# An eight-core decoder layer: norm steps at an even rate, weight copies paused in two stages, and stores moved to ScalarE's queue

## The chip, the cores and the metric

The kernel runs on all 8 cores of one Trainium2 chip. The sequence of 8192 tokens is cut into 8 parts, and each core computes the whole layer for its 1024 tokens (plus a small halo). The cores don't talk to each other. The metric is the device time of the slowest core, in microseconds (us). Cores 0 to 3 are one die, 4 to 7 the other.

In some of its executions this program has a second, slower state: the cores of one die, or of both, show a lower granted TensorE clock (the share of full speed that the chip allows TensorE; no view here shows more than 1.00) and the time is longer. Fast runs are compared with fast runs here. TensorE = PE in the profile (PEld its weight loads), VectorE = DVE, ScalarE = ACT, GpSimd = POOL, SyncE = SP. A name such as ACTq is the queue of that engine in which DMAs are issued. A DMA lands when the profile shows it done; "us to landing" counts from its issue. PSUM (`ps` in the profile) is the memory into which TensorE's matmuls write here, in banks that VectorE and ScalarE then read (892 and 291 instructions in the two largest such groups of the kernel before).

## The reference, cut to what matters

```python
for i in range(DEPTH):                                # DEPTH = 1, D_MODEL 4096, D_FF 11008
    h = rms_norm(x, norm_mix_pre[i]);  z = h @ w_in[i]
    q, k, v, u, g_attn, g_pool = jnp.split(z, split_points, axis=-1)
    # ... attention with window 128, pooling mixer ...
    merged = jax.nn.sigmoid(g_attn) * y_attn + jax.nn.sigmoid(g_pool) * y_pool
    x = x + rms_norm(merged @ w_out[i], norm_mix_post[i])             # output projection, norm, residual
    h = rms_norm(x, norm_ffn_pre[i])
    up = causal_depthwise_conv(h @ w_up[i], conv_w[i], conv_b[i])     # up-projection
    gate, val = jnp.split(up, 2, axis=-1)
    x = x + rms_norm((jax.nn.gelu(gate, approximate=True) * val) @ w_down[i], norm_ffn_post[i])
    ple_gate = jax.nn.sigmoid(rms_norm(x, norm_ple_gate[i]) @ w_ple_gate[i])      # the gate
    x = x + rms_norm(ple_gate * (p[i] @ w_ple[i]), norm_ple_post[i])
```

Inputs and output are fp32; the kernel multiplies in bf16 and accumulates in fp32. Each `x = x + rms_norm(...)` is a run of 32 norm steps, one for each block of 128 channels.

## The kernel before

The kernel is a list of jobs, which are matmul groups over one output block of 128 channels. Near the output projection, the down-projection's end and the gate, each stage is cut into two parts of tokens: "part 0" (the first 512) and "part 1". While TensorE works on one part, the norm steps of the other are put between its matmuls. A queue named `side` holds these steps, and a job takes one off it after every `side` matmul groups:

```python
            cnt = 0                                    # in run_jobs, anew for every job
            ...
                    cnt += 1
                    if side and cnt // side > (cnt - 1) // side and self.side:
                        self.side.popleft()()
```

So with 32 groups per job and `side` 12, a job takes 2 steps, and the remaining 8 groups are forgotten. What is left in the queue runs in one lump at `B.code(B.drain_side)`.

One norm step, cut:

```python
        def main(k):
            m, x, r = src[k], S["x"][k % NR], S["r"]          # NR = 4 buffers for the residual
            O("dve", "tensor_tensor", ..., out=m.v, in0=m.v, in1=r, op=ALU.mult)
            O("dve", "scalar_tensor_tensor", ..., in1=x.v, ...)   # gain, plus the residual x
            ld_(k + NR)                                       # SyncE: next residual load
            put(k, m)                                         # SyncE: store of the new x (or of out)
            if hout is not None:
                O("act", "activation", ..., func=AF.Square)   # q
                O("act", "activation", ..., func=AF.Copy)     # h, input of the next matmuls
        def step(k):
            def run():
                if k < NCH:
                    main(k)
                if hout is not None and k >= 2:
                    ss(k - 2)                                 # TensorE: sum of the squares of step k - 2
```

Weights come in slabs of up to 8 x 128 x 128, which GpSimd loads as bf16 into a ring of 12 (`sb_wr`). Beside the slabs GpSimd also issues copies: weights that are read twice are turned from fp32 in memory (`w_out`, ...) to bf16 in memory (`b_out`, ...), one copy of 1 MB for every 8 slabs:

```python
        self.O("pool", "dma_start", [cast] if cast else [], [self.wringB[i]], dma=f"wr{i}", ...)
        if self.casting and self.nload % 8 == 0:
            self.cast_next()
```

All waits are worked out from reads and writes. A write marked `partial` still waits for every earlier writer of the same record, and all stores to `out` share one record (`outB`) and one counter:

```python
        for b in writes:
            for d in (b.w, b.r):                  # also with partial=True
                for k, v in d.items():
                    deps[k] = max(deps.get(k, 0), v)
    ...
    O("sp", "dma_start", [m.b], [outB], partial=True, dma="out", out=out_d[k][:, t0:t0 + 512], in_=m.v)
```

The gated mixer tiles `mg` that did not fit into on-chip memory are loaded back by SyncE at the end of the mixer gates, once `h0` and `r0` are free.

The softmax here doesn't subtract the row's maximum and nothing guards it: scores larger than these inputs give would overflow.

## Time and profile before

| | before |
|---|---|
| runs beside the changed kernel | 7069.54, 7080.66, 7090.2 us fast; 7908.45 slow |
| profiled run, spans of the cores | 7037.4 to 7086.9 us, core 7 slowest |
| mean granted clock | 0.966 to 0.972 |
| TensorE busy (core 7) | 6628.3 us, 94% |
| DMA moved (core 7) | 910.65 MB |

The lines of this profile stand in the prediction below.

### The profile page before, as it was taken

Reading aid. Unit: us, or ns where it says so; the run is one execution under the profiler, and the core shown is the slowest. Engines: PE = TensorE matmul, PEld = TensorE weight load, DVE = VectorE, ACT = ScalarE, POOL = GpSimd, SP = SyncE. Lnnn points to the kernel's source line nnn. Section 1 sums busy time; section 2 is a strip of 40 time slices with the busy share of each in tenths; the row PEclk is TensorE's granted clock in tenths of the full one; section 3 lists DMA queues with packets and bytes.
Section 4 is the critical chain, followed back from the end, with each engine's and each line's share of the span. In section 5 each row is a group of like instructions: output and inputs, shape, how many; then the busy total and the mean of one; then the engine's idle time right before and its main releaser. Section 6 shows DMA issues by size and latency. Waiting matters only on the chain.

```text
span 7086.9 us, 104514 instructions; the slowest of 8 cores (7037.4 to 7086.9 us)
## 1 busy us (share of the span) xinstructions
PE 6628.3 (94%) x41282; PEld 4048.3 (57%) x41282; DVE 1984.6 (28%) x2553; ACT 823.3 (12%) x1242; POOL 1335.2 (19%) x2501
## 2 busy tenths in 40 slices
PE   5999999999999787899999999999999999997865
PEld 3656666666664563666654566664456666443332
DVE  3343211111110213433310133331023333244334
ACT  2550000000001222100000000000000000133111
POOL 1111111111113222211111111111111111332321
PEclk8999999999999888899999999999999999998987
DMA  6457877777789999844456644447864444686563
GB/s 162 77 80 109 119 113 114 120 117 118 114 150 207 203 198 196 174 76 76 76 102 118 114 76 76 76 76 141 160 114 76 76 76 93 203 267 206 163 205 120
DMA packets 377375, 910.65 MB, mean 128 GB/s; under 512 B 50176, under 2 KB 72960, under 8 KB 371328
## 3 DMA queue, kind: packets, MB, share of 16 engines
q0 software_dynamic: 289344, 705.33, 57.3%
q1 hardware_dynamic: 87552, 198.64, 9.2%
q8 instruction: 337, 5.52, 0.3%
q14 instruction: 142, 1.16, 0.1%
HBM read 1297.47 MB, written 200.32 MB: 211 GB/s over the span
## 4 chain that ended last, share of the span: by engine, by line
PE 86%; DMA 9%; DVE 2%; ACT 1%; issue 1%; POOL 0%; DVEq 0%; SPq 0%; ACTq 0%; POOLq 0%
PE ps L143 86%; DMA sb_arena<-xr 5%; DVE sb_arena L143 2%; DMA out<-sb_arena 1%; ACT sb_arena L143 1%; DMA sb_arena<-w_in 1%; DMA sb_arena<-x_s 1%; DMA sb_wr<-b_out 1%; DMA sb_arena<-mg_s 1%; DMA sb_arena<-xs 0%; POOL sb_arena L143 0%; DVEq L142 0%; ACT L143 0%; ACTq L142 0%; SPq L143 0%
## 5 line engine op out<-in xcount | busy, mean ns | idle before, releaser
L143 PE MATMUL ps<-sb_arena,sb_wr 128*128 128x512 bf16 (+5 forms) x39744 | 6440.1, 324 | 101.3 <-DVE sb_arena L143 79.0
L143 PEld LDWEIGHTS ps<-sb_arena,sb_wr 128*128 128x128 bf16 x39744 | 3906.6, 99 | 2549.7 <-issue 137.0
L143 DVE TENSOR_TENSOR sb_arena<-ps,sb_arena 128x512 f32<-128x512 f32 (+9 forms) x892 | 682.1, 765 | 4066.7 <-PE ps L143 3868.9
L143 ACT ACTIVATE sb_arena<-sb_arena 128x512 f32<-128x512 f32 (+10 forms) x683 | 493.0, 725 | 4921.1 <-DVE sb_arena L143 4803.9
L143 POOL DMA_DIRECT2D sb_wr<-w_up x632 | 333.7, 528 | 1839.7 <-PE ps L143 1715.3
L143 DVE TENSOR_TENSOR sb_arena<-sb_arena 128x512 f32<-128x512 f32 (+8 forms) x543 | 452.0, 841 | 546.8 <-ACT sb_arena L143 518.9
L143 DVE SCALAR_TENSOR_TENSOR sb_arena<-sb_arena,sb_convp 128x1024 f32<-128x1024 f32 (+2 forms) x372 | 447.9, 1204 | 39.5 <-DVE sb_arena L143 0.9
L143 POOL DMA_DIRECT2D sb_wr<-w_in x384 | 204.3, 533 | 1308.6 <-PE ps L143 1308.6
L143 PE MATMUL ps<-sb_arena,sb_ones_b 128*128 128x296 bf16 (+3 forms) x288 | 87.4, 389 | 243.7 <-ACT sb_arena L143 217.8
L143 POOL DMA_DIRECT2D sb_wr<-w_down x256 | 135.2, 528 | 675.1 <-PE ps L143 624.1
L143 ACT ACTIVATE sb_arena<-ps 128x512 bf16<-128x512 f32 (+7 forms) x291 | 159.8, 549 | 788.6 <-PE ps L143 782.1
L143 DVE SCALAR_TENSOR_TENSOR sb_arena<-sb_arena,sb_gains 128x512 f32<-128x512 f32 (+1 forms) x192 | 144.7, 753 | 283.2 <-DMA sb_arena<-xr 204.0
L143 POOL DMA_DIRECT2D sb_wr<-b_out x256 | 138.2, 540 | 443.2 <-PE ps L143 440.2
L143 PE MATMUL ps<-sb_arena 128*128 128x296 bf16 (+4 forms) x1216 | 183.6, 273 | 27.5 <-DVE sb_arena L143 16.2
L143 POOL DMA_DIRECT2D sb_wr<-b_pg x256 | 137.4, 537 | 358.3 <-PE ps L143 342.7
L143 PEld LDWEIGHTS ps<-sb_arena,sb_ones_b 128*128 128x128 bf16 x288 | 27.3, 105 | 293.7 <-issue 282.7
L143 POOL DMA_DIRECT2D sb_wr<-b_down x256 | 137.4, 537 | 281.2 <-PE ps L143 245.1
L143 PEld LDWEIGHTS ps<-sb_arena 128*128 128x128 bf16 (+1 forms) x1216 | 110.3, 100 | 105.7 <-issue 71.2
L143 DVE TENSOR_SCALAR sb_arena<-sb_arena,sb_convp 128x1024 f32<-128x1024 f32 (+2 forms) x186 | 143.8, 773 | 20.9 <-DVE sb_arena L143 0.9
L143 POOL DMA_DIRECT2D sb_wr<-b_up x112 | 60.6, 541 | 239.0 <-PE ps L143 239.0
L143 ACT ACTIVATE sb_arena<-sb_arena,sb_gains 128x512 bf16<-128x512 f32 (+1 forms) x128 | 90.7, 708 | 0.0
L143 POOL DMA_DIRECT2D sb_wr<-w_bp x64 | 33.8, 528 | 194.2 <-PE ps L143 190.7
(34 smaller groups left out, 390.7 us busy)
## 6 DMA issues: line engine op xcount, KB each, us to landing
sb_wr<-w_up POOLq DMA_DIRECT2D x632, 256.0 KB, 4.3
sb_wr<-w_in POOLq DMA_DIRECT2D x384, 256.0 KB, 5.5
sb_wr<-b_out POOLq DMA_DIRECT2D x256, 256.0 KB, 11.9
sb_wr<-b_pg POOLq DMA_DIRECT2D x256, 256.0 KB, 3.0
sb_wr<-w_down POOLq DMA_DIRECT2D x192, 256.0 KB, 4.1
sb_wr<-b_down POOLq DMA_DIRECT2D x192, 256.0 KB, 3.8
b_out<-w_out POOLq DMA_DIRECT2D x32, 1024.0 KB, 13.0
b_pg<-w_pg POOLq DMA_DIRECT2D x32, 1024.0 KB, 18.5
```

The source lines that it names most:

```text
L143: inst = getattr(engine, fn[0])(**fn[1])
```

## The change

The intent is to keep TensorE from standing behind norm steps: no lumps, no weight copies beside the residual traffic of the two stages where it is dense, and SyncE's queue freed of stores. The diff, cut to its core:

```diff
@@ run_jobs
+        self.due = 0
-            cnt = 0
-                    cnt += 1
-                    if side and cnt // side > (cnt - 1) // side and self.side:
-                        self.side.popleft()()
+                    if side:
+                        self.due += 1 / side
+                        if self.due >= 1:
+                            self.due -= 1
+                            if self.side:
+                                self.side.popleft()()
@@ last mixer gate
-                                O("sp", "dma_start", [mgdB[c]], [t.b], ...)
+                                O("sp" if c % 2 else "pool", "dma_start", [mgdB[c]], [t.b], ...)
@@ evac of out_job, down_part and e_job (three places)
+                    B.drain_side()
                     B.side.extend(bar1(hf, G["acc"]))
@@ put of bar1, bar2 and last
-                O("sp", "dma_start", [m.b], [x1B[hf][k]], ...)
+                O("act", "dma_start", [m.b], [x1B[hf][k]], ...)
@@ before the output projection, and after the partial up-projection
+        B.code(casting(False))
...
+        B.code(casting(True))
@@ after down_part(1, ...), after the gate's part 0 and after its part 1
-        B.code(B.drain_side)
@@ tail
-                O("sp", "dma_start", [m.b], [outB], partial=True, dma="out", ...)
+                O("sp" if f % 2 else "act", "dma_start", [m.b], [outB], partial=True, dma="out", ...)
```

Half of the `mg` loads move to GpSimd. And the record `outB` stays, so each store to `out` still waits for the one before it, whichever queue it stands in.

More of the change, by code (lines that the diff above doesn't have):

```diff
@@ L268, in load_next @@
         self.nload += 1
+        assert cast is None or cast.w, wname
         src = self.dram[wname][off:off + nk * 16384].rearrange("(p m) -> p m", p=128)
@@ L733, in evac @@
                             if c in mgdB:
-                                O("sp", "dma_start", [mgdB[c]], [t.b], dma=f"mgl{c % 8}", out=t.v, in_=mg_d[c])
+                                O("sp" if c % 2 else "pool", "dma_start", [mgdB[c]], [t.b], dma=f"mgl{c % 8}", out=t.v, in_=mg_d[c])
             B.one(B.chunk(banks, NCH, rhs_e, rb_h0, evac), B.slabs("w_in", 36 + which * 32 + f, NCH))
@@ L912, in put @@
                 t0 = 0 if hf == 0 else 510
-                O("sp", "dma_start", [m.b], [x1B[hf][k]], dma=f"x1s{k % 8}", out=x1_d[k][:, t0:t0 + n - a],
+                O("act", "dma_start", [m.b], [x1B[hf][k]], dma=f"x1s{k % 8}", out=x1_d[k][:, t0:t0 + n - a],
                   in_=m.v[:, a:n])
@@ L923, in bar1, with casting, run @@
             return norm_steps(n, blocks, mix[hf], lambda: acc, 1, res, put, 2, h1[hf], rn)
+        def casting(on):
+            def run():
+                B.casting = on
+            return run
+        B.code(casting(False))
         for f in range(NCH):
@@ L1076, in evac @@
                         free([G["a"].pop(base[2] + k) for k in range(K3)], G["yin"])
+                    B.drain_side()
                     B.side.extend(bar2(hf, G["acc"]))
@@ L1090, in put @@
             def put(k, m):
-                O("sp", "dma_start", [m.b], [x2B[hf][k]], dma=f"x2s{k % 8}", out=x2_d[k][:, t0:t0 + 512], in_=m.v)
+                O("act", "dma_start", [m.b], [x2B[hf][k]], dma=f"x2s{k % 8}", out=x2_d[k][:, t0:t0 + 512], in_=m.v)
             def rn():
@@ L1144, in evac_e @@
                     free(G["sqf"], [h2[hf][c] for c in range(NCH)])
+                    B.drain_side()
                     if hf == 0:
@@ L1160, in put @@
             def put(k, m):
-                O("sp", "dma_start", [m.b], [outB], partial=True, dma="out", out=out_d[k][:, t0:t0 + 512], in_=m.v)
+                O("act", "dma_start", [m.b], [outB], partial=True, dma="out", out=out_d[k][:, t0:t0 + 512], in_=m.v)
             return norm_steps(512, ((0, 512),), R3[hf], lambda: acc, 5, res, put, None, None, lambda: None)
@@ L1179, in build_nc @@
             e_job(0, f, 14)
-        B.code(B.drain_side)
         for f in range(NCH):
             e_job(1, f, 14)
-        B.code(B.drain_side)
         def tail():
@@ L1195, in tail @@
                   scalar=gains[:, 5, f:f + 1], in1=x.v, op0=ALU.mult, op1=ALU.add)
-                O("sp", "dma_start", [m.b], [outB], partial=True, dma="out", out=out_d[f][:, 512:1024], in_=m.v)
+                O("sp" if f % 2 else "act", "dma_start", [m.b], [outB], partial=True, dma="out", out=out_d[f][:, 512:1024], in_=m.v)
         B.code(tail)
```

## The prediction

> **What bounds the kernel now.** I read the page's slices first, then the list of cores, then what TensorE waited for, then a table of stretches that I cut at the stage borders, and last the DMA issues and SyncE's queue in the stretches that stood out. The page, part 2, 40 slices of 177 us each:
>
> ```profile
> PE   5999999999999787899999999999999999997865
> PEclk8999999999999888899999999999999999998987
> DMA  6457877777789999844456644447864444686563
> ```
>
> TensorE is the bound: 6628.3 us busy in a span of 7086.9 (94%). The missing 459 us sit in a few places: the first slice (loading x, which the change leaves alone), slices 13 to 16, and the last four. In slices 13 to 16 the granted clock is low too, and the DMA engines are at 9. The table of stretches (columns: us, busy us and instructions of each engine, granted clock, DMA share, GB/s moved):
>
> ```profile
> 2109.00:2337.50 228.50, 220.95 (x1001) 98.37 (x1001) 20.77 (x30) 38.61 (x63) 75.06 (x140) 0.98 1.00 207
> 2337.50:2684.50 347.00, 281.28 (x2082) 223.93 (x2081) 65.18 (x96) 81.61 (x133) 77.22 (x144) 0.83 0.95 198
> 2684.50:2883.50 199.00, 122.39 (x515) 52.99 (x516) 86.91 (x128) 47.80 (x77) 34.56 (x64) 0.81 0.97 201
> 2883.50:3600.00 716.50, 715.16 (x5123) 502.09 (x5121) 279.89 (x328) 32.13 (x35) 124.51 (x236) 1.00 0.54 91
> 6180.00:6385.00 205.00, 205.00 (x950) 92.97 (x948) 86.30 (x126) 61.49 (x98) 64.93 (x121) 1.00 0.85 260
> 6385.00:6452.50 67.50, 21.51 (x40) 4.26 (x38) 46.11 (x68) 44.19 (x71) 6.95 (x13) 0.54 0.93 296
> 6452.50:6692.00 239.50, 236.17 (x1089) 106.68 (x1087) 65.53 (x95) 42.98 (x68) 85.75 (x160) 0.99 0.55 154
> 6692.00:6790.00 98.00, 23.11 (x104) 10.27 (x104) 44.17 (x66) 2.60 (x3) 8.04 (x15) 0.63 0.66 186
> ```
>
> The rows are: output projection, part 0; output projection, part 1, with the norm steps of part 0 (2337 to 2684); partial up-projection, part 0, with the norm steps of part 1 (2684 to 2883); the rest of the up-projection's first stretch; down-projection, part 1, with its norm steps; a hole; the embedding gate, part 0; a hole. Each hole is a lump: all remaining norm steps run at once, and TensorE stands behind them.
>
> Why are the two stages at 2337 and 2684 slow? The DMA issues of 2684 to 2885 say it (issuer, count, size, us to landing), and the same view of the down-projection, part 1, says what such a transfer takes without weight copies:
>
> ```profile
> x_s<-sb_arena SPq DMA_DIRECT2D x32, 257.0 KB, 24.4
> sb_arena<-xr SPq DMA_DIRECT2D x31, 261.0 KB, 24.2
> b_pg<-w_pg POOLq DMA_DIRECT2D x7, 1024.0 KB, 19.5
> ...
> sb_arena<-x_s SPq DMA_DIRECT2D x32, 256.0 KB, 4.9
> ```
>
> A norm step needs one load of the residual and there are four buffers for it: at most 4 loads per 24.2 us, a step per 6.0 us, 32 steps in 194 us. The stages lasted 347 and 199 us, the second nearly this limit. TensorE waited 131.8 us on ScalarE's squares between 2109 and 2900, 34 times: the sum-of-squares matmul of step k-2 stands in TensorE's order, so late steps stop it. The copies (fp32 weights in memory to bf16 in memory, 1 MB each) are what fills the DMA engines: 201 GB/s already makes a share of 0.97, while 260 GB/s without copies makes 0.85.
>
> [...] issue is small: about 0.32 us for a load and 0.4 for a store on SyncE. [...] the holes show 0.54 and 0.63, and 2575 to 2675 on this core shows 0.81 without idling, which cores 0 to 5 do not.
>
> **The change, part by part.**
>
> *Copies paused.* 110 copies exist, one per 8 weight slabs. Before the output projection 528 slabs are issued, so 66 copies, enough for its own 32 and the 14 of the partial up-projection. The other 44 move behind the partial stages, into the up-projection, where DMA is at 0.5 to 0.6. The early stages (775 to 2074) carry copies beside the same kind of weight loads with TensorE busy 1298 of 1299 us, so there they cost nothing.
>
> Output projection, part 1: 2048 matmuls of 264 or 258 columns. At full clock 227 of these take 25 us (the later stage 2925 to 2950), 0.110 us each: 225.5 us, plus 32 sum-of-squares matmuls at 0.22 us and the first reduction, 8 us: 234. Demand: 1 MB of weights per 7.05 us job plus two steps of 0.52 MB, 296 GB/s, near what the lump at 6385 moved. I add 9 us of stalls: 243 against 347, **104 us**.
>
> Partial up-projection, part 0: 448 matmuls of 512 columns at 0.218 us make 98, plus 64 small ones at 0.11, 106 us. The even rate (a step per 12 matmul groups carried across jobs, 2.67 per job instead of 2, then a lump) fits all 35 pieces into the 14 jobs and removes the 31 us lump. But demand is 1 MB + 1.38 MB per 7 us, 347 GB/s, over what this chip showed, and VectorE has 87 us of work here. I estimate 119 us against 199: **80 us**.
>
> Output projection, part 0 waited on b_out and on the gate tiles some 10 us; half of those tiles now come through GpSimd. I count **7 us**.
>
> *Lump at 6385.* The drain after the down-projection goes; 35 pieces spread over the gate's 32 jobs at 32/14 = 2.29 per job. Removed 67.5 us, and about 8.5 us of small matmuls move into the next stage. There demand is 154 + 2.29 x 0.52 MB per 7.3 us = 318 GB/s for 15 jobs; I allow 8 us of stalls. **51 us**.
>
> *Lump at 6692.* TensorE waited 74.6 us for VectorE in one piece; with the clock's restart, 77. Now the 57 pieces (34 steps, 22 loads) spread over the gate, part 1. But here ScalarE's stores matter. The stores to "out" share one counter, and the code makes each wait until the previous one has landed. SyncE's queue in the last stretch shows it:
>
> ```profile
> 7015.02 69.86 SPq L143 DMA_DIRECT2D out<-sb_arena  x32
> ```
>
> 32 stores in 69.86 us, 2.18 each, with a landing of 2.0: one at a time. In the gate stage such a store, now in ScalarE's order ahead of the next sigmoid, will take 4 to 5 us to land (4.9 to 5.2 for its like at a share of 0.85), against a step each 3.2 us. 14 jobs then fall behind by 14 x (2.29 x 4.5 - 7.3) = 42 us, of which the PSUM banks (six, three jobs) absorb some 17. Loss 25, gain **52 us**.
>
> *Tail stores half from ScalarE.* The chain store after store holds across engines, since each still waits for the one before it. VectorE needs 32 x 1.52 = 49 us, the stores 70. **0 us**, though the intent is a gain of 20.
>
> *Stores of other norm steps from ScalarE.* Their counters rotate over eight; 0.4 us of ScalarE's time each, 64 + 64 of them, on an engine at 12%: 0 by itself.
>
> Sum: 104 + 80 + 7 + 51 + 52 = 294. 7080.66 - 294 = 6787, say 6788.
>
> **Rivals.**
> 1. The copies were not the cause; the norm traffic itself saturates DMA. For it: demands of 296 to 347 GB/s against the 296 at a share of 0.93 seen. Against it: landings of 4.9 us at 260 GB/s. The two stages would then fall to perhaps 290 and 150 us, total about 6870.
> 2. ScalarE's queue turns against the weights: [...] TensorE waits for weights instead of squares. Speaks for it that 12 slabs are only three jobs of slack. Some 30 us more, 6820.
> 3. ScalarE's serial "out" stores stop the gate, part 1, fully: landing 6 us would give back the 52 us, 6840. Against: the landing in the lump was 3.0 us, and with that the loss is 0, total 6763.
> 4. The tail does overlap after all: 20 us less, 6768.
> 5. [...] 340 us at 0.81 cost 80 more, 6868. Against: the dense stages show 1.00 on all cores.
>
> **Range and chances.** With no stall anywhere the sum of floors is 6741; lower is hardly possible unless the tail overlaps. With the stalls doubled it is about 6840. So 6735 to 6860 for 8 in 10. Even rival 1 stays under 6939, the 2% mark; the lumps alone bring 103 us, 1.5%, and any shortening of the DMA-bound stages does the rest. Faster 0.97, same 0.03, slower 0.
>
> **What would show it.** Right: residual loads landing in 5 to 10 us instead of 24; no hole at 6385 and 6692; clock near 1.00 between the output projection and the up-projection; the up-projection with copies still at full TensorE; last stores at 2.2 us steps on two queues; ScalarE waiting on "out" stores late in the gate stage. Wrong: residual loads still above 15 us, TensorE waiting on weight slabs, a tail of 55 us, or TensorE gaps in the up-projection where the copies went.

## More of the kernel before

To compare stages across kernels I cut TensorE's timeline at marks that every version has: the fp32 reduction with which a run of norm steps starts, and the last sum-of-squares matmul. The stages of the kernel before, on its slowest core, are in the table of the result.

## The result

| | before | after |
|---|---|---|
| fast runs, us | 7069.54, 7080.66, 7090.2 | 6829.7, 6840.38 |
| slow runs, us | 7908.45 | 6968.39 (die 0), 7069.98 (die 1) |
| profiled run, slowest core | 7086.9 | 6827.9 |
| granted clock | 0.966 to 0.972 | 0.986 to 0.988 |

The ratio is 0.9654, with a 95% interval of 0.9616 to 0.9692: faster. A ratio here is the mean time of one kernel's fast runs over that of the other's in the same rounds, so it is not quite the ratio of medians. With means of 7080.1 and 6835.0 us the gain is 245 us; 294 were predicted.

By stages, on the slowest core of each profile (core 7 before, core 2 after):

| stage | before | after | difference | predicted |
|---|---|---|---|---|
| start to the end of output projection part 0 | 2341.0 | 2350.8 | +9.8 | -7 |
| output projection, part 1 | 346.8 | 239.0 | -107.8 | -104 |
| partial up-projection, part 0 | 195.6 | 120.6 | -75.0 | -80 |
| rest, to the down-projection's part 1 | 3306.0 | 3308.3 | +2.3 | 0 |
| down-projection, part 1 | 201.6 | 200.9 | -0.7 | 0 |
| gate, part 0 (with the lump before it) | 301.4 | 247.8 | -53.6 | -51 |
| gate, part 1 (with the lump before it) | 315.9 | 287.1 | -28.8 | -52 |
| tail | 78.7 | 73.3 | -5.4 | 0 |

The differences sum to 259.2 us, the difference of the two spans up to rounding.

The slices of the page, part 2, for the changed kernel (40 slices of 171 us):

```profile
PE   5999999999998998999999999999999999999975
PEclk8999999999999999999999999999999999999997
DMA  6446776777665678666689855557865554588683
```

Counted from 1 (the prediction counted from 0), slices 14 to 17 of PE had been 7, 8, 7 and 8; now 13 and 16 show an 8 and the rest 9. The four 8s of the granted clock there are gone, and so is the dip in slice 37. DMA no longer shows four 9s in a row. Slices 18 to 23 had been 4 to 6 and are now 6 to 9: that is where the copies went.

The same table of stretches as in the prediction (us; busy us and instructions of PE, PEld, DVE, ACT, POOL; granted clock; DMA share; GB/s), for the changed kernel's core 2:

```profile
2120.00:2347.50 227.50, 225.61 (x1044) 103.90 (x1063) 23.23 (x32) 38.72 (x64) 69.69 (x130) 1.00 0.53 158
2347.50:2587.00 239.50, 235.28 (x2065) 203.11 (x2079) 65.17 (x96) 83.04 (x133) 68.36 (x129) 1.00 0.77 207
2587.00:2711.00 124.00, 105.64 (x480) 48.30 (x491) 82.34 (x122) 47.64 (x76) 28.32 (x53) 0.96 0.98 247
2711.00:3430.00 719.00, 713.27 (x5063) 503.27 (x5145) 283.84 (x334) 32.45 (x35) 136.51 (x258) 1.00 0.69 118
...
6219.00:6467.00 248.00, 242.53 (x1102) 109.59 (x1122) 108.12 (x160) 84.98 (x135) 86.30 (x161) 1.00 0.72 213
6467.00:6754.00 287.00, 243.83 (x1056) 107.16 (x1078) 107.54 (x160) 44.18 (x68) 78.79 (x147) 0.94 0.69 200
6754.00:6828.00 74.00, 1.10 (x2) 0.30 (x2) 43.74 (x65) 2.60 (x3) 0.00 (x0) 0.51 0.30 114
```

Compare the first number of PE with the length of the stretch. In the output projection, part 1, TensorE is busy 235.28 of 239.5 us, where it had been busy 281.28 of 347. The row at 2711 has the paused copies beside it, and TensorE is still busy 713 of 719 us. The gate's part 0 is almost full too. The two rows that are not are the partial up-projection at 2587 and the gate's part 1 at 6467, with 43 us missing.

The DMA issues of the row at 2587, between 2590 and 2711 us (what was written and read, issuer, count, size, us to landing):

```profile
sb_wr<-b_up POOLq DMA_DIRECT2D x52, 256.0 KB, 9.7
x_s<-sb_arena ACTq DMA_DIRECT2D x32, 257.0 KB, 13.6
sb_arena<-xr SPq DMA_DIRECT2D x29, 261.0 KB, 13.5
```

A residual load lands in 13.5 us instead of 24.2. The DMA engines are still full (share 0.98), but 247 GB/s now get through instead of 201.

Two new waits came in. The first lies before the output projection. GpSimd's timeline (start us, us, what it did, and in brackets how long it stood before and what released it):

```profile
2076.87 1.10 POOL L143 DMA_DIRECT2D sb_arena<-mg_s  x2 [39.16 <-DVE sb_arena L143]
...
2082.53 0.54 POOL L143 DMA_DIRECT2D sb_arena<-mg_s  x1 [3.13 <-DMA sb_arena<-mg_s]
...
2092.37 0.54 POOL L143 DMA_DIRECT2D sb_wr<-w_ba  x1 [0.21 <-issue]
```

And TensorE's timeline on the same core:

```profile
2098.69 31.54 PE L143 MATMUL ps<-sb_arena,sb_wr 128*128 128x344 bf16 x189 [20.31 <-DMA sb_wr<-w_ba]
```

GpSimd stood for 39.16 us before its first `mg` load, which goes into memory that VectorE still uses. Then it stood again between these loads. The weight slabs of `w_ba` are behind them in the same queue, so TensorE ran out of slabs and stood 20.31 us. On the eight cores this wait is 18.8 to 22.4 us.

The second is in the gate's part 1. What ScalarE and TensorE waited for between 6460 and 6760 us (us in total, times, longest):

```profile
ACT sb_arena L143 <- DMA out<-sb_arena: 128.9, 13, 24.3
ACT sb_arena L143 <- DVE sb_arena L143: 115.3, 52, 5.1
...
PE ps L143 <- DVE sb_arena L143: 43.1, 13, 10.5
```

ScalarE stood 128.9 us on stores to `out`. A sigmoid that stands behind such a store is late, VectorE waits for it before it empties the PSUM bank (133.8 us on ScalarE in the same window), and TensorE waits for VectorE: 43.1 us, which with 243.83 us of work makes the 287 us of the stage. The chain that ended last runs through these stores, one after the other (start us, us):

```profile
6600.49 5.33 DMA out<-sb_arena
6605.88 9.21 DMA out<-sb_arena
6615.16 8.79 DMA out<-sb_arena
6624.01 8.33 DMA out<-sb_arena
```

In the tail, two queues now hold 16 stores each (timelines of SyncE and of ScalarE):

```profile
6762.44 63.52 SPq L143 DMA_DIRECT2D out<-sb_arena  x16
6760.34 63.53 ACTq L143 DMA_DIRECT2D out<-sb_arena  x16
```

They lie side by side, but 32 stores from 6760.34 to 6825.96 are 2.05 us for each: still one at a time, against 2.18 before.

### The profile page after: what moved, and what is told of

The parts are those of the page before. It is cut to its first block, busy times and chain, and to the rows that moved or that the text cites.

```text
span 6827.9 us, 104052 instructions; the slowest of 8 cores (6791.8 to 6827.9 us)
## 1 busy us (share of the span) xinstructions
PE 6537.4 (96%) x40781; PEld 4025.8 (59%) x41282; DVE 1982.2 (29%) x2553; ACT 825.9 (12%) x1244; POOL 1339.9 (20%) x2511
## 4 chain that ended last, share of the span: by engine, by line
PE 90%; DMA 5%; DVE 2%; ACT 1%; issue 1%; POOL 0%; ACTq 0%; DVEq 0%; POOLq 0%; SPq 0%
PE ps L143 90%; DVE sb_arena L143 2%; DMA out<-sb_arena 1%; DMA sb_arena<-xr 1%; ACT sb_arena L143 1%; DMA sb_arena<-w_in 1%; DMA sb_arena<-xs 0%; DMA sb_wr<-b_out 0%; POOL sb_arena L143 0%; DMA sb_arena<-mg_s 0%; DMA sb_wr<-w_ba 0%; DVEq L142 0%; ACTq L143 0%; ACTq L142 0%; ACT L143 0%
## 5 line engine op out<-in xcount | busy, mean ns | idle before, releaser
L143 PE MATMUL ps<-sb_arena,sb_wr 128*128 128x512 bf16 (+6 forms) x39260 | 6376.0, 322 | 95.8 <-DVE sb_arena L143 43.0
L143 PE MATMUL ps<-sb_arena,sb_ones_b 128*128 128x296 bf16 (+3 forms) x271 | 69.2, 343 | 89.7 <-ACT sb_arena L143 89.4
```

The costliest lines, as they stand in the source:

```text
L143: inst = getattr(engine, fn[0])(**fn[1])
```

## The experiments

All twelve gave correct results. "Same chip" means the same call: chips differ in the clock and time of the kernel before (its fast runs took 7065.0 us in the mean, with core clocks of 0.970 to 0.973, beside the controls, and 7118.5 us with 0.958 to 0.972 beside p1_pause), while the changed kernel took 6835.0 and 6836.2 us in two calls. So stage lengths and same-chip differences carry the argument, not the small differences of ratios.

**One part alone.** These three put one part of the change into the kernel before; a fourth takes one part out of the change.

*p1_pause*, the kernel before with the copies paused:

```diff
+        B.code(casting(False))
         for f in range(NCH):
             out_job(0, f, 0)
...
         for j in range(RU):
             up_part(1, j, 0)
+        B.code(casting(True))
```

> The kernel before with only the pause of the weight copies. My theory: the copies are what holds the residual loads at 24 us, so the output projection, part 1, falls from 347 to 240 to 250 us and the partial up-projection, part 0, from 199 to 130 to 145 us (its lump of seven pieces stays), both 60 us holes stay; 6900 to 6930 us in all. Rival (the queue on ScalarE and the even rate did most of it, the copies were a bystander): both stages stay over 300 and 180 us, total above 7020.

Measured: 6893.3 us (mean of 4 fast) against 7118.5 on the same chip, ratio 0.9684 [0.9647, 0.972]. The output projection's part 1 took 239.8 us and the partial up-projection 123.7, the rest 3305.0. The gate's parts stayed long, 303.1 and 325.8. Residual loads landed in 14 to 15.3 us. The partial up-projection fell further than the 130 to 145 us expected (114 to 124 us over the cores; 99 to 121 in the full change). So the pause alone makes both stages nearly what they are in the full change, and the moved copies cost nothing where they went. The gain of 225 us is more than the 107 + 72 which these stages show against the recorded profile of before; the kernel before was slower on this chip than on the first one by some 38 us, and it was not profiled there.

*p2_even*, the kernel before with the even rate and the drains only: the accumulator `due`, `drain_side` before each new run of steps, and four drains dropped.

> The kernel before with only the even rate and the drains removed; stores stay on SyncE, copies go on. My theory: the holes of 67 and 77 us go, but the gate, part 1, stalls by 25 to 50 us on the serial out stores, and the DMA-bound stages stay near 347 and 199 us: 6980 to 7010 us. Rival (evenness alone cures the DMA-bound stages as well): below 6930.

Measured: 6997.3 us, ratio 0.983 [0.9739, 0.992]. The profile says more. The first two stages stayed at 323.1 and 186.1 us. The lumps went, but cores 2 to 5 had a granted clock of 0.81 in the gate. The four cores at full clock took 243.5 us for part 0 and 248 to 254 us for part 1. The stores to `out` are one at a time here as well, but they stand in SyncE's queue: on core 0, from 6718 to 6967 us, SyncE waited 108.9 us on them and TensorE only 12.2 us on VectorE. So the stall of 25 to 50 us that was expected in part 1 did not come on these cores, and the total hit the expected 6980 to 7010 us by luck: one of the three fast runs, the profiled one of 7049.21 us, had the lower clock instead. This was the first sign that one-at-a-time stores do harm only through ScalarE.

*p3_act*, the kernel before with the stores moved only:

```diff
-                O("sp", "dma_start", [m.b], [x1B[hf][k]], ...)        # and x2, and out
+                O("act", "dma_start", [m.b], [x1B[hf][k]], ...)
-                O("sp", "dma_start", [m.b], [outB], partial=True, dma="out", ...)       # tail
+                O("sp" if f % 2 else "act", "dma_start", [m.b], [outB], partial=True, dma="out", ...)
```

> The kernel before with only the stores moved to ScalarE's queue (norm steps, half of the tail). My theory: the stores to out stay one at a time across both queues (2.2 us each, tail 75 to 78 us), the other stores were never the wait: within 0.3% of before, 7060 to 7100 us. Rival (SyncE's queue was crowded: its loads stood behind its stores): residual landings fall and the total falls by 50 us or more, and the tail loses 20 us.

Measured: two fast runs, 7105.22 and 7113.62, against 7118.5, a ratio of 0.9987 without an interval; four of six runs were slow. Stages: 326.8, 194.5, 306.1, 342.7, and the tail 79.3. No gain shows, and the gate's part 1 became longer: 342.7 against 315.9, and 333 to 343 on all cores against 309 to 323. What TensorE waited for between 2340 and 2960 us changed:

```profile
PE ps L143 <- DMA sb_wr<-b_out: 65.2, 23, 8.2
PE ps L143 <- DMA sb_wr<-b_up: 43.6, 12, 10.7
PE ps L143 <- ACT sb_arena L143: 26.6, 6, 6.7
```

The same view of the kernel before:

```profile
PE ps L143 <- ACT sb_arena L143: 131.8, 34, 13.1
PE ps L143 <- DMA sb_wr<-b_out: 10.5, 3, 7.8
```

With a third busy queue the residual loads of the output projection's part 1 land sooner (16.0 us instead of 25.2), the weight slabs later (23.6 instead of 12.8), and TensorE waits for slabs instead of squares.

*e3_copies_on*, the changed kernel without the pause (the two `casting` lines taken out):

> The changed kernel without the pause. My theory: residual landings return to about 24 us, the two stages to about 330 to 350 and 190 to 200 us: 6990 to 7030 us. Rival [...]: stages of 280 and 160 us, total 6890 to 6930, with TensorE waiting on weight slabs instead.

Measured: 7037.4 us against 7118.5, ratio 0.9886 [0.9832, 0.994]. The two stages are long again on every core looked at: 326.5 and 182.8 us on core 7, 314 to 338 and 169 to 190 on die 0. The gate's parts, 247.9 and 289.3, are those of the full change. TensorE's waits between 2330 and 2950 us:

```profile
PE ps L143 <- DMA sb_wr<-b_out: 72.2, 19, 8.9
PE ps L143 <- ACT sb_arena L143: 69.3, 29, 7.8
```

(On this core the output projection's part 1 begins at 2427 us; from there on both waits are 64.7 us.) The residual loads did not go back to the expected 24 us. The DMA issues of the output projection's part 1, 2427 to 2753 us:

```profile
sb_wr<-b_out POOLq DMA_DIRECT2D x115, 256.0 KB, 24.2
sb_arena<-xr SPq DMA_DIRECT2D x28, 256.0 KB, 14.6
```

In p1_pause the same loads landed in 15.3 us and the slabs in 6.9, and the stage took 239.8 us instead of 326.5. So a quick landing of the residual loads does not make the stage short; here the slabs are late instead.

So the even rate and ScalarE's queue do nothing for these stages without the pause.

**What cost time in the change.** These four ran on one chip, with the kernel before at 7093.1 us.

*e1_mg_sp*, the changed kernel with all `mg` loads on SyncE again:

```diff
-                                O("sp" if c % 2 else "pool", "dma_start", [mgdB[c]], [t.b], ...)
+                                O("sp", "dma_start", [mgdB[c]], [t.b], ...)
```

> The changed kernel with all twenty gate-tile loads issued by SyncE, as before. My theory: GpSimd's queue stood 39 us behind a wait on VectorE for the tiles' memory, the weight slabs behind it, and TensorE waited 20.3 us for w_ba; that wait goes, and the total falls by 18 to 25 us (6805 to 6820 for fast runs). Rival (the DMA engines are simply full there with the tiles): the wait only moves to mg tiles, gain under 8 us.

Measured: 6838.6 us (mean of 2 fast), ratio 0.9641 [0.96, 0.9683], which cannot be told from the changed kernel's on another chip; 6805 to 6820 were expected. Its profile fell in the slow state of die 1, so only die 0 counts: spans of 6773.2 to 6810.5 us where the changed kernel's die 0 had 6804.5 to 6827.9. The first stage fell from 2350.8 to 2321.8 us on core 2, and by 24 us in the mean of die 0 (2347.1 to 2323.3), and the wait of TensorE for `w_ba` is gone. The whole time does not show the gain; the stage does.

*e2_out_free*, the changed kernel with a record of its own for each store to `out`, and counters over 8:

```diff
-        outB = Buf("out")
+        outB = [[Buf(f"out{p}_{c}") for c in range(NCH)] for p in range(2)]
-                O("act", "dma_start", [m.b], [outB], partial=True, dma="out", out=..., in_=m.v)       # last
+                O("act", "dma_start", [m.b], [outB[0][k]], dma=f"ou{k % 8}", out=..., in_=m.v)
-                O("sp" if f % 2 else "act", "dma_start", [m.b], [outB], partial=True, dma="out", ...)  # tail
+                O("sp" if f % 2 else "act", "dma_start", [m.b], [outB[1][f]], dma=f"ov{f % 8}", ...)
```

> The changed kernel with a counter rotating over eight and a buffer record of its own for each out store, so that none waits for the one before. My theory: the gate, part 1, loses its 43 to 52 us of stalls behind ScalarE and the tail falls from 73 to 53 to 56 us (VectorE's 49 us and one landing): 60 to 70 us less, 6765 to 6775. Rival (the gate's part 1 is held by DMA bandwidth with the 22 extra loads, not by the order of stores): the tail gains 18 us and the gate part under 15.

Measured: 6783.6 us, ratio 0.9564 [0.9502, 0.9625], a little over the 6765 to 6775 expected; in two of its three fast runs cores of die 0 had a lower clock (0.983 to 0.987 where the others had 0.990 to 0.991). The gate's part 1 and the tail (windows and SyncE's timeline):

```profile
6492.00:6734.00 242.00, 233.65 (x1056) 104.75 (x1078) 108.60 (x159) 44.18 (x68) 78.80 (x147) 1.00 0.82 236
```

```profile
6741.89 46.17 SPq L143 DMA_DIRECT2D out<-sb_arena  x16
```

The stage fell from 287.1 to 242.2 us and the tail from 73.3 to 55.7, with SyncE's stores done in 46 us instead of 63.5. Both losses therefore come from the shared record and its one counter (the edit changes both at once).

*e4_both*, e1 and e2 together:

> Both mends. My theory: they lie in different stages and add: 6740 to 6755 us for fast runs. Rival (what one frees is lost again in the next stage): less than 65 us under the changed kernel.

Measured: 6745.5 us, ratio 0.951 [0.9482, 0.9538]. It is 38.1 us faster than e2_out_free on the same chip, and the only difference in the code is who loads `mg`. Not all of the 38.1 us is due to it: the one fast run of e2_out_free without a lower clock took 6762.53 us, 17 more. In the profile of e4_both the first stage takes 2325.9 us. In that of e2_out_free it took 2374.9 on the slowest core, at a granted clock of 0.92 between 500 and 900 us; on the six cores without this it took 2339.9 to 2350.3, against 2317.1 to 2326.2 on all cores of e4_both. So the loads are worth some 23 us.

*e5_aligned*, e4 with the residual input laid out so that each row starts at a multiple of 64 bytes: two arrays with rows of 512 and of 528 fp32 values instead of one with 1026 (4104 bytes). The second array holds columns 504 to 1025, so its tile starts at a row's start as well.

```diff
-    xr_d = din("xr", [NCH, 128, NE])
+    xr_d = [din("xr0", [NCH, 128, 512]), din("xr1", [NCH, 128, 528])]
-                O("sp", "dma_start", [], [t.b], ..., in_=xr_d[k][:, lo:lo + n])
+                O("sp", "dma_start", [], [t.b], ..., in_=xr_d[hf][k][:, 0:n])
```

> Both mends, and the residual x laid out in two arrays whose rows start at multiples of 64 bytes (before: rows 4104 bytes apart). In the changed kernel these loads cost 5.9 us of one sixteenth share per MB against 3.2 for the loads of the later norm stages whose rows are 4096 bytes apart, and land in 13 us against 5.8. My theory: the row starts cause it; landings fall under 8 us, the DMA share of the partial up-projection falls below 0.95, that stage falls from 124 to 108 to 114 us, total 6725 to 6742. Rival (the loads are dear because three queues are full, whatever the rows): landing and stage stay, total as e4.

Measured: 6725.2 us, ratio 0.9481 [0.9454, 0.9509], 20 us faster than e4_both on the same chip. The DMA issues of the partial up-projection (2562 to 2669 us), and its row in the windows of e5_aligned:

```profile
x_s<-sb_arena ACTq DMA_DIRECT2D x32, 257.0 KB, 10.4
sb_arena<-xr SPq DMA_DIRECT2D x30, 261.0 KB, 10.4
```

```profile
2562.00:2669.00 107.00, 99.21 (x477) 46.42 (x474) 81.47 (x120) 46.47 (x74) 27.91 (x52) 0.98 0.97 281
```

The same of e4_both (2562 to 2684 us):

```profile
sb_arena<-xr SPq DMA_DIRECT2D x29, 261.0 KB, 14.0
```

```profile
2562.00:2684.00 122.00, 101.20 (x468) 46.03 (x476) 81.63 (x121) 46.78 (x74) 27.57 (x52) 0.97 0.87 244
```

Loads land in 10.4 us instead of 14.0, and 281 GB/s get through instead of 244. The landing under 8 us and the DMA share under 0.95 that were expected did not come; the stage became shorter all the same. The stage takes 106.8 us on the slowest core and 100 to 107 on all, where e4_both had 100 to 123. This version is the fastest of all, 110 us under the changed kernel's fast runs (on another chip).

**Controls.** *a0_again* is the changed kernel once more, and *b1_aligned* is the kernel before with e5's layout of the residual; *e6_no_act* is e4 with every store back on SyncE (each `"act"` of a store becomes `"sp"`). They shared a chip, with the kernel before at 7065.0 us.

> The changed kernel itself once more, so that it stands beside the others on one chip. Both theories: fast runs at 0.960 to 0.970 of before, the gate, part 1, at 285 to 292 us.

Measured: 6836.2 us, ratio 0.9675 [0.9656, 0.9694]. It confirms the first result: 6835.0 there. The gate's part 1 took 287 to 297 us over the cores.

> The kernel before with only the residual x laid out in aligned rows, copies going on. My theory: the copies hold the DMA engines, the row starts are a second-order cost: landings fall from 24 to about 20 us, the two stages to about 300 and 175 us, total 7020 to 7060. Rival (the row starts were the cause of the slow stages all along): landings near 8 us, stages near 245 and 120 us, total near 6900.

Measured: 7058.7 us, ratio 0.9991 [0.9949, 1.0033], the same. Residual loads landed in 22 to 25 us, as before; the fall to 20 that was expected did not come. So the layout shows no gain with the copies going on (DMA share of the two stages 0.95 and 0.97 in the profile of the kernel before; the interval leaves room for half a per cent). In this profile the output projection's part 1 took 306 to 317 us on the cores, not 346.8; the kernel before itself was not profiled on this chip.

> Both mends, but with every store back on SyncE's queue. My theory: ScalarE's queue is worth nothing once the out stores don't wait for each other (issue takes SyncE 0.3 to 0.4 us each): total within 0.3% of the kernel with both mends (ratio to before 0.948 to 0.954), tail 54 to 57 us. Rival (a second queue is what makes the loads quick): the gate's stages lose 10 us or more each, ratio above 0.956.

Measured: 6738.7 us, ratio 0.9537 [0.9515, 0.9558]. The stages are 238.8, 123.4, 243.5, 237.1 and the tail 56.8. Against e4_both's 0.951 the intervals overlap. Once a store waits for no other store, the whole time does not show whether ScalarE or SyncE issues it. By stage small differences remain, between two chips: the gate's part 0 took 243.5 us on all eight cores here and 247.8 to 247.9 in e4_both, while the partial up-projection took 120 us in the mean of the cores here and 115 there.

*e7_last_sp* is the changed kernel with the stores to `out` of the gate's part 1 (not the tail's) back on SyncE, still one at a time:

```diff
-                O("act", "dma_start", [m.b], [outB], partial=True, dma="out", out=out_d[k][:, t0:t0 + 512], ...)
+                O("sp", "dma_start", [m.b], [outB], partial=True, dma="out", out=out_d[k][:, t0:t0 + 512], ...)
```

> The changed kernel with one word changed: the out stores of the last norm steps that run beside the gate, part 1, are issued by SyncE again, still each waiting for the one before. Theory (the harm is that ScalarE's own order stops behind a waiting store, so the sigmoids behind it come late): the gate, part 1, takes 245 to 260 us instead of 284 to 294 at full clock, the tail stays at 73 to 85 us, total 6795 to 6810 for fast runs. Rival (stores one at a time hold the stage whichever engine issues them): the stage stays at 280 us or more and the total at 6825 to 6845.

Measured: 6817.4 us against 7109.2, ratio 0.9596 [0.9536, 0.9655]; 6795 to 6810 were expected, and in two of the three fast runs two cores had a lower clock (0.982 to 0.984). The gate's part 1 took 242.3 to 253.9 us on cores 0 to 5 (clock 0.97 to 1.00). Cores 6 and 7 took 273 us at a clock of 0.88 in that stretch, and TensorE waited only 4.8 and 5.6 us on VectorE there. What SyncE and TensorE waited for in that stage on core 2:

```profile
SPq L142 <- DMA out<-sb_arena: 99.6, 32, 5.1
```

```profile
PE ps L143 <- DVE sb_arena L143: 10.7, 6, 3.9
```

SyncE waited 99.6 us on stores, TensorE 10.7 on VectorE instead of 43.1. The stores are as serial as before; only the queue they stand in has changed. Behind a waiting store in ScalarE's queue stands the next sigmoid. Behind one in SyncE's stand only residual loads, for which four buffers are there.

## Why the prediction was right, and where it was not

**Copies paused: right.** Predicted were 104 and 80 us, measured 107.8 and 75.0, and p1_pause alone and e3_copies_on show that the pause is the cause. Three things in the working were off. First, it had late residual loads alone hold the stages, a norm step per 6.0 us, and named their landing as the sign to watch. With the copies on, the weight slabs can be the late ones just as well: in e3_copies_on the residual loads land in 14.6 us and the stage still takes 326.5, as the slabs take 24.2. The pause makes both kinds of loads land sooner than in the kernel before: 15.3 and 6.9 us in the output projection's part 1 of p1_pause, against 25.2 and 12.8, and the DMA share of that stage is 0.95 before and 0.77 after the change. Second, the residual loads were to land in 5 to 10 us; they took 12 to 13.5. In the partial up-projection the DMA engines are still full (share 0.98) at 247 GB/s, against the demand of 347 in the working. Third, the 80 us were counted from a stretch of 199 us, where the stage by its marks is 195.6; its new length was met, 119 predicted and 120.6 measured. That stage lasted 116 to 121 us on five cores and 98 to 99 on cores 0, 5 and 7, so rival 1 is partly true there. And the 104 us hold for the slowest core of one profile, which had a clock of 0.82 there: on the eight cores of that profile the stage took 309 to 349 us before and 236 to 239 after, so the gain is 73 to 113 us.

**The moved copies: right.** "Rest" is 3304 to 3310 us on the slowest core of every profile, with the copies there or not.

**Gate tiles through GpSimd: failed, in sign.** The prediction counted 7 us gained for the output projection's part 0, as its waits on `b_out` and on the gate tiles were to shrink. The measured stage ended 9.8 us later. The step only asked which queue has less to do and not what stands behind a load that has to wait. The first load stood 39.16 us on VectorE, and with it the weight slabs; TensorE stood some 20 us. With the loads back on SyncE the stage is 2322 to 2326 us (e1_mg_sp, e4_both). So the pause did bring 13 to 19 us there (p1_pause, which has the pause alone, took 2328.4), and the tiles cost some 24 us, 25 to 29 on the slowest cores.

**Lump at 6385: right,** 51 predicted, 53.6 measured.

**Lump at 6692: right in its mechanism, wrong in size.** The prediction had ScalarE stand behind the serial stores, with 25 us of loss and 52 of gain. The gain was 28.8 us. The term that was mis-sized is the loss: the changed stage took 287.1 us where e2_out_free needs 242.2 without the serial wait, so about 45 us. The estimated landing of 4.5 us was good for most stores (4.4 measured), but three near the end took 8 to 9 us, so that the mean of the 32 is 4.7. By the prediction's own sum that makes a loss of some 31 us with the slack of 17 and 48 without, so the slack was less than assumed; it was an estimate, and no run varied it. The restart of the clock that the prediction counts with this lump is in the trace of the kernel before: core 7's granted clock is 0.50 from 6750 to 6790 us, with TensorE idle, 0.82 from 6790 to 6798 and 1.00 from 6798 to 6806. In the trace a burst of residual loads, the 22 kept ones among them, is issued from 6602 to 6640 us, where these three stores stand. That the burst makes them slow is argued from this only; no run took those loads away. The alternative, that serial stores as such cost the time, fell with e7_last_sp and p2_even: serial on SyncE, the stage takes 242 to 254 us.

**Tail: right.** 0 predicted, and the stores still follow each other at 2.05 us. The 5.4 us of this profile are within what the same kernel shows otherwise: its tail is 84.9 us in a0_again. Two queues alone bring nothing; freed of the shared record, the tail is 55.7 us. Rival 4 is thus what the change would have brought with e2's edit.

**Stores of the other norm steps on ScalarE: right by the sum, with rival 2 seen on the way.** p3_act shows no gain, and e6_no_act no loss in the whole time. While copies run, TensorE does wait for weights once ScalarE issues stores, as rival 2 had it, whose 30 us were an estimate (in the output projection's part 1 the slabs land in 23.6 us in p3_act instead of 12.8, and the waits on `b_out` are 10.5 us before, 63.0 and 64.7 in p3_act and e3_copies_on), but in p3_act the waits on ScalarE shrink by about as much as those on slabs grow (131.8 to 26.6 us over the two stages).

**Clock: right.** The mended stages show 1.00 and 0.96, and rival 5's further 340 us at 0.81, an estimate too, did not come in the changed kernel's fast runs (mean clock 0.986 to 0.988 on every core).

Together: 259.2 us of the predicted 294 show in the profiles. The missing 35 are 17 of the gate tiles, 23 of the lump at 6692, 5 of the partial up-projection and 2 to 3 of the rest, less 12 to 13 for the places that did better (4 in the output projection's part 1, 3 at 6385, 5 in the tail).

**Open.** Why the clock of 0.81 comes to some cores and not to others is not known; it makes up a part of before's time in the two stages, which I cannot separate. e1_mg_sp by its whole time did not beat the changed kernel, though its stage was some 24 us shorter; e1 and the changed kernel did not run on one chip.

## What to carry to other kernels

Before you move a DMA to another engine's queue, list what stands behind it there, and ask what the DMA itself waits for: a store that waits for another store did little harm here in a queue that holds only prefetched loads (TensorE waited 10.7 us in the gate's part 1 of e7_last_sp), and cost compute in the queue of an engine on the path (43.1 us in the changed kernel). When transfers in a stage are slow, first take away the traffic that could run elsewhere, and only then spread queues or align rows: here the first was worth most of the gain (107.8 and 75.0 of the 259.2 us in the profiles), and alignment was worth 20 us after it (e5_aligned) and showed nothing before it (b1_aligned, 0.9991). Two queues do not overlap if a shared record and its counter tie their transfers together: in the tail 32 stores on two queues still took 2.05 us each. And a load that lands sooner is no gain yet: look at what lands later for it (in p3_act the residual loads landed in 16.0 us instead of 25.2, the slabs in 23.6 instead of 12.8).

## What these runs show of queues, rows and the clock

- A DMA that has to wait holds the work behind it on its issuer. The gate's part 1 took 287.1 us with serial stores on ScalarE and 242.3 to 253.9 on SyncE at a clock of 0.97 to 1.00 (e7_last_sp). On GpSimd, tile loads of which the first waited 39.16 us held the weight slabs, and TensorE stood 18.8 to 22.4 us.
- With one more issuing queue, the transfers of another queue landed later: with copies running, the slabs of the output projection's part 1 landed in 23.6 us (p3_act) instead of 12.8, and TensorE's waits on `b_out` there rose from 10.5 to 63.0 us (64.7 in e3_copies_on).
- With rows of 4104 bytes replaced by rows of 2048 and 2112, loads in the partial up-projection landed in 10.4 instead of 14.0 us, 20 us in all; with copies going on, no gain showed (ratio 0.9991). The runs show that the layout matters, not why.
- In the kernel before, all eight cores ran dense from 775 to 2074 us (1298 to 1299 us busy) at 1.00; from 2575 to 2675 us cores 6 and 7 showed 0.81 and the others 0.98 to 1.00. In the profiled run of p2_even, between 6460 and 6680 us, cores 2 to 5 showed 0.81 while cores 0 and 1 of the same die, and 6 and 7 of the other, showed 1.00. In e7_last_sp only cores 6 and 7 showed 0.88 in the gate's part 1, and in e2_out_free only cores 2 and 3 showed 0.92 between 500 and 900 us (0.99 to 1.00 on the others). So in these profiles of fast runs the lower clock comes to cores by twos and not by dies; no run shows why.
